# Partial sums of a seven-product block multiplication kept in PSUM instead of added on VectorE

## The chip, the cores and the metric

The kernel runs on one core of a Trainium2 chip. A core has a matrix engine (TensorE, in the profile PE for the matmuls and PEld for the loading of their weights), three engines for element-wise work (VectorE is DVE, ScalarE is ACT, GpSimd is POOL), and an engine that issues DMAs (SyncE, SP). Matmul results land in PSUM, which DVE and ACT read in this kernel; POOL works on SBUF alone. The metric is the device time of one execution in microseconds. Three runs of the kernel before took 1466.47 to 1467.98 us, median 1466.99 us.

## What is computed

The reference is a two-layer network on 1024 latent tokens (and 256 context tokens) of width 1024. What matters here are four matrix products, each of which the kernel does with one scheme:

```python
# layer 0, second half of the output projection's input comes from branch A
x  = x + gate * (concat([y_a, y_b]) @ ev_w_out)     # y_a part: "woa"
# layer 1 (w_grp and scale are folded with the first half of od_w_in)
u, g = split(h @ od_w_in)                           # "v" (folded) and "g"
y  = group_matmul(pool(u) - u, w_grp) * scale * silu(g)
x  = x + gate * (y @ od_w_out)                      # "wo": two halves of the 2048 inputs, "wo0" and "wo1"
out = rmsnorm(x, final_g)
```

## The kernel before

**Tiles.** Channels lie on the 128 partitions, tokens along the free dimension. A number in fp32 is split into a rounded high part and a low rest, and a product is three matmuls (high x high, high x low, low x high) of 128 x 128 weights on 128 x 512 data.

**A quad.** `quad` (L610) makes two output row tiles (m and m + 1) of all 1024 tokens, so four blocks of 128 x 512: (0,0), (0,1), (1,0) and (1,1), row tile and token half. Input and weight are cut in halves too, and a Strassen scheme in Winograd's form makes the four blocks from seven products instead of eight: products 1 to 7 take the operands `b11`, `b21`, `b22`, `t4`, `t1`, `t2`, `t3` in that order of their numbers. Each product is 12 matmuls (`prod`, L595), a quad is 84. Blocks are sums of products: (0,0) is 1 + 2, and the other three share the partial sum 1 + 6, and two of them also 1 + 6 + 7.

Before, the shared sums are made outside PSUM: ACT copies product 1 to an SBUF tile `s1` (L616); DVE adds product 6 to it into `s2` (L621) and product 6 + 7 to it into `s1` (L636); product 2 is accumulated on product 1 in PSUM tile `a`, product 7 on 6 in `b`, product 3 on 5 in `c`, and product 4 has its own tile `d`. ACT copies product 5 to `s3` (L629). Then `put` ends each block: (1,1) is `s3 + s1`, added on POOL; (1,0) is `s1 - d`, (0,1) is `s2 + c`, added on DVE. `quad` is called 26 times, for woa (4), v (8), g (8), wo0 (4) and wo1 (2), and the last two quads of wo1 have the same pattern written out in `last_half0` (L1182) and after it.

**What put does.** For v (`to_tokens`, L1011) it leaves the block in a tile that is pooled along the tokens on DVE; for g (`to_gate`, L1018) ACT applies SiLU, and DVE multiplies the two (L1057); for woa and wo0 (`added`, L802) DVE multiplies by the gate and adds the residual, which a DMA loads into one of two buffers (`xp`) and another stores; for the other quads of wo1 (`put`, L1102) the residual is already in SBUF (`gated`, L1090).

**Weights.** For each quad `wquad` (L567) loads two raw tiles (two buffers), makes the combinations that the seven products need, and splits each into high and low: ACT casts the high part (L94), DVE makes the low part of products 1 and 6, POOL of 2, 5, 7, 4 and 3 (L95). So the raw tiles of the next quad are loaded when POOL has done with those of the last one, and the loads stand in SP's queue between the stores of the results.

**Operands.** The operands of wo0 and wo1 are sums of y blocks that go through DRAM (`y_store` L952, `y_sums`, `y_operand` L969).

**Order.** A planner, not the source, sets the order of each engine's instructions: it simulates the program, starts what is ready, and prefers what has high priority (`tc.high_priority`, the readers of PSUM) or comes earlier in the source; `tc.issue_after` adds an order on one engine. Each engine then runs its list in that order. PSUM has four tiles for `a`, `b`, `c`, `d` (pool `pm`).

Of the kernel before, what the change touches and what calls it, by code (L numbers as in the profile page):

```python
# [20 lines left out]
KT = D // P  # L21
H = 512
# [28 lines left out]
BOPS = ("b11", "t2", "b21", "t1", "t3", "t4", "b22")  # L51
# [3 lines left out]
def body(ctx, tc, xT, ctxT, cc, ccol, modT, modW, win, gw, wout, wu, grp, wg, wo1, small, edge, ident, outT):  # L55
# [511 lines left out]
    def wquad(src, name, ring):  # L567
        raw = []
        for i in range(2):
            r = wpool.tile([P, D], F32, tag="wr", name=f"wr_{name}_{i}")  # L570
            loaded[0] = nc.sync.dma_start(r, src[i])
# [9 lines left out]
        p1 = op(a11, 1, nc.vector)  # L581
        s3 = ttile(f"ws_{name}")
        nc.vector.tensor_tensor(out=s3, in0=a11, in1=a21, op=sub)
        nc.vector.tensor_tensor(out=a21, in0=a21, in1=a22, op=add)
        nc.vector.tensor_tensor(out=a11, in0=a21, in1=a11, op=sub)  # L585
        p6 = op(a11, 6, nc.vector)
        p2 = op(a12, 2, nc.gpsimd)
        p5 = op(a21, 5, nc.gpsimd)
        p7 = op(s3, 7, nc.gpsimd)
        nc.vector.tensor_tensor(out=a12, in0=a12, in1=a11, op=sub)  # L590
        p4 = op(a22, 4, nc.gpsimd)
        p3 = op(a12, 3, nc.gpsimd)
        return p1, p2, p3, p4, p5, p6, p7
# [13 lines left out]

    EVAC = 1000

    def quad(w, name, ops, put, ahead=None):  # L610
        p1, p2, p3, p4, p5, p6, p7 = w
        a = psum(f"qa_{name}")
        prod(a, p1, ops["b11"], True, False)
        s1 = ttile(f"s1_{name}")
        with tc.high_priority(offset=EVAC):
            evac_a = nc.scalar.copy(s1, a)  # L616
        b = psum(f"qb_{name}")
        prod(b, p6, ops["t2"], True, False)
        s2 = ttile(f"s2_{name}")
        with tc.high_priority(offset=EVAC):  # L620
            evac_v = nc.vector.tensor_tensor(out=s2, in0=b, in1=s1, op=add)  # L621
# [3 lines left out]
        c = psum(f"qc_{name}")  # L625
        prod(c, p5, ops["t1"], True, False)
        s3 = ttile(f"s3_{name}")
        with tc.high_priority(offset=EVAC):
            nc.scalar.copy(s3, c)  # L629
        w = None  # L630
        if ahead is not None:
            with tc.issue_after(evac_a.ins), tc.issue_after(evac_v.ins):
                w = ahead()
        prod(b, p7, ops["t3"], False, True)
        with tc.high_priority(offset=EVAC):
            nc.vector.tensor_tensor(out=s1, in0=b, in1=s1, op=add)  # L636
# [4 lines left out]
        with tc.high_priority(offset=EVAC):  # L641
# [123 lines left out]
    for i in range(KH):  # L765
# [16 lines left out]
        nc.vector.tensor_tensor(out=t4, in0=t2, in1=b21, op=sub)  # L782
        split_op(ya, "t2", i, t2)
        split_op(ya, "t1", i, t1)
        for name, v in zip(BOPS[4:], (t3, t4, b22)):
            kept[name].append(v)
# [13 lines left out]


    def added(gate, m, i, h, x, y, op, dst=None):  # L802
        t = vtile(f"xp{m}_{i}_{h}")
        dst = t if dst is None else dst
        nc.sync.dma_start(t, x1_part[m + i][:, HALF[h]])
        if y is not None:
            eng = nc.gpsimd if (i, h) == (1, 1) else nc.vector
            eng.tensor_tensor(out=x, in0=x, in1=y, op=op)
        nc.vector.scalar_tensor_tensor(out=dst, in0=x, scalar=gate[:, 0, 2 * KT + m + i : 2 * KT + m + i + 1],  # L809
                                       in1=t, op0=mult, op1=add)  # L810
        nc.sync.dma_start(x1_part[m + i][:, HALF[h]], dst)
# [18 lines left out]
    def woa(m, w, ahead):  # L830
        def put(i, h, x, y, op):
            if (i, h) == (0, 0):
                for q in range(2):
                    x1[m + q] = xtile(f"x1_{m + q}")
            v = x1[m + i][:, HALF[h]]
            added(m0, m, i, h, x, y, op, v)
            square_acc(nacc[h][:, :H], v, (m, i) == (0, h), f"n1q{m}_{i}_{h}")
# [57 lines left out]
    for i in range(KH):  # L895
# [3 lines left out]
        t = block_sums(b11, b12, b21, b22, ttile(f"xt3_{i}"), nc.vector)  # L899
        split_x("t2", i, t["t2"], shift(KH + i), None)  # L900
        split_x("t1", i, t["t1"], None, nc.gpsimd)
        split_x("t3", i, t["t3"], dsh[:, i : i + 1], None)
        split_x("t4", i, t["t4"], None, nc.gpsimd)
        split_x("b22", i, b22, shift(KH + i), None)
# [46 lines left out]

    def y_store(m, name, v):  # L952
        part, i = divmod(m // 2, KH)
        nc.sync.dma_start(y_raw[part][name][:, i * H : (i + 1) * H], v)
# [9 lines left out]
    def y_sums(m):  # L964
        t = block_sums(*y_blocks(m), vtile(f"yt3_{m}"), nc.vector)
        for name in BOPS[1:2] + BOPS[3:6]:
# [30 lines left out]
    def wo1_weights(part, m):  # L997
        return wquad([wo1[m + i, part] for i in range(2)], f"wo{part}_{m}", wo1_ring)

    wo1_ring = wo_ring(iter(["x", "x", "x", "wh", "wl", "wh", "wl"] + ["wh", "wl", "d", "d"] * 14))  # L1000
    vps = []
    for m in range(0, NK, 2):
# [8 lines left out]
        def to_tokens(i, h, x, y, op):  # L1011
            if y is None:
                nc.scalar.copy(token[i][h], rows(x))
            else:
                eng = nc.gpsimd if (i, h) == (1, 1) else nc.vector
                eng.tensor_tensor(out=token[i][h], in0=rows(x), in1=rows(y), op=op)

        def to_gate(i, h, x, y, op):  # L1018
            v = ys[m + i][:, HALF[h]]
            if y is None:  # L1020
                nc.scalar.activation(v, x, AF.Silu)
            else:
                eng = nc.gpsimd if (i, h) == (1, 1) else nc.vector
                eng.tensor_tensor(out=v, in0=x, in1=y, op=op)
                nc.scalar.activation(v, v, AF.Silu)
# [22 lines left out]
        def first_weights():  # L1048
            w = wo1_weights(0, 0)
            y_operands(0, iter([xtile] * 7), BOPS[4:])  # L1050
            return w

        w = quad(wq, f"g{m}", bx, to_gate, first_weights if m == NK - 2 else None)
# [16 lines left out]

    for m in range(0, KT, 2):
        def put(i, h, x, y, op):
            added(m1, m, i, h, x, y, op)
# [16 lines left out]
    def gated(k, v, x):  # L1090
        return nc.vector.scalar_tensor_tensor(out=v, in0=x, scalar=m1[:, 0, 2 * KT + k : 2 * KT + k + 1],  # L1091
                                              in1=v, op0=mult, op1=add)

# [7 lines left out]
    for m in range(0, KT - 4, 2):  # L1101
        def put(i, h, x, y, op):  # L1102
            v = x1[m + i][:, HALF[h]]
            if y is not None:
                eng = nc.gpsimd if (i, h) == (1, 1) else nc.vector
                eng.tensor_tensor(out=x, in0=x, in1=y, op=op)
            gated(m + i, v, x)
            square_fin(m + i, h, slice(0, H), v)
# [73 lines left out]
    def last_half0(m, w, ahead=None):  # L1182
        p1, p2, p3, p4, p5, p6, p7 = w
        a = psum(f"qa_l{m}")
        prod(a, p1, ops["b11"], True, False)
        s1, s2 = ttile(f"s1_l{m}"), ttile(f"s2_l{m}")
        with tc.high_priority(offset=EVAC):
            evac_a = nc.scalar.copy(s1, a)
        b = psum(f"qb_l{m}")
        prod(b, p6, ops["t2"], True, False)  # L1190
        with tc.high_priority(offset=EVAC):
            evac_v = nc.vector.tensor_tensor(out=s2, in0=b, in1=s1, op=add)
        nxt = None
        if ahead is not None:
            with tc.issue_after(evac_a.ins), tc.issue_after(evac_v.ins):
                nxt = ahead()
        prod(a, p2, ops["b21"], False, True)
        with tc.high_priority(offset=EVAC):
            gated(m, x1[m][:, HALF[0]], a)
            fin_add(HALF[0], square(m, HALF[0]))  # L1200
        mm = prod(b, p7, ops["t3"], False, True)
        with tc.high_priority(offset=EVAC):
            gated(m, x1[m][:, HALF[1]], s2)
            nc.vector.tensor_tensor(out=s1, in0=b, in1=s1, op=add)
        d = psum(f"qd_l{m}")
        with tc.issue_after(mm.ins):
            mm = prod(d, p4, ops["t4"], True, True)
        with tc.high_priority(offset=EVAC):
            nc.vector.tensor_tensor(out=d, in0=s1, in1=d, op=sub)
            gated(m + 1, x1[m + 1][:, HALF[0]], d)  # L1210
            fin_add(HALF[0], square(m + 1, HALF[0]))
            vec = gated(m + 1, x1[m + 1][:, HALF[1]], s1)
# [143 lines left out]
```

## Time and profile before

| what | value |
|---|---|
| median of three runs | 1466.99 us |
| the profiled execution, its own time | 1463.63 us |
| its span, first to last instruction | 1461.8 us |
| mean granted TensorE clock | 0.961 |
| instructions of PE, DVE, ACT, POOL in the trace | 5664, 1445, 906, 398 |

The span falls into stages, by what TensorE works on: up to 763 us the projections and the recurrence of layer 0, which the change leaves alone; 763 to 854 the four quads of woa; 854 to 906 the folding of weights and the normalisation; 906 to 1254 the sixteen quads of v and g in eight pairs; 1254 to 1401 the four quads of wo0 and two of wo1; 1401 to 1445 the last two quads of wo1, and then the final normalisation. In a row of groups the columns are line, engine, operation, output <- inputs, shapes, count, then busy microseconds and mean nanoseconds of one, then idle time before it. In a row for a stretch they are the stretch, its length, and busy microseconds with the count for each engine, then the granted clock, the share of DMA time, and GB/s.

### The profile page before, as it was taken

Reading aid. Unit: us, or ns where it says so; the run is one execution under the profiler, and the core shown is the slowest. Engines: PE = TensorE matmul, PEld = TensorE weight load, DVE = VectorE, ACT = ScalarE, POOL = GpSimd, SP = SyncE. Lnnn points to the kernel's source line nnn. Section 1 sums busy time; section 2 is a strip of 40 time slices with the busy share of each in tenths; the row PEclk is TensorE's granted clock in tenths of the full one; section 3 lists DMA queues with packets and bytes.
Section 4 is the critical chain, followed back from the end, with each engine's and each line's share of the span. In section 5 each row is a group of like instructions: output and inputs, shape, how many; then the busy total and the mean of one; then the engine's idle time right before and its main releaser. Section 6 shows DMA issues by size and latency. Waiting matters only on the chain. (4 is left out here: it accounts for less than half of the span.)

```text
span 1461.8 us, 15892 instructions
## 1 busy us (share of the span) xinstructions
PE 1323.3 (91%) x5664; PEld 1060.8 (73%) x5664; DVE 1265.6 (87%) x1445; ACT 639.2 (44%) x906; POOL 739.9 (51%) x398
## 2 busy tenths in 40 slices
PE   7799989897999889999998989999998997798896
PEld 4478767776777677888886877778777775577675
DVE  7985889798879899997878859999999999986985
ACT  6443584466457624226334345433332223433542
POOL 5273654664557456425327446555435536445642
PEclk9999999999999999999999999999999999899998
DMA  9741212121211223443542475133342135457723
GB/s 362 251 116 39 63 37 73 65 65 34 75 51 52 71 94 119 133 146 120 190 137 98 158 219 169 56 129 129 116 137 86 66 116 173 151 187 241 244 91 115
DMA packets 82867, 181.80 MB, mean 124 GB/s; under 512 B 7778, under 2 KB 27618, under 8 KB 82788
## 3 DMA queue, kind: packets, MB, share of 16 engines
q1 hardware_dynamic: 74340, 176.60, 36.7%
q10 hardware_dynamic: 8448, 4.20, 1.0%
q8 instruction: 44, 0.72, 0.2%
q14 instruction: 35, 0.29, 0.1%
HBM read 136.72 MB, written 44.04 MB: 124 GB/s over the span
## 5 line engine op out<-in xcount | busy, mean ns | idle before, releaser
L681 DVE SCALAR_TENSOR_TENSOR conv<-u,sm,conv 128x1009 f32<-128x1009 f32 (+14 forms) x240 | 300.8, 1272 | 21.9 <-ACT conv L674 18.7
L95 POOL TENSOR_TENSOR wl_wu<-wr_wu,wh_wu 128x1024 fp32r<-128x1024 f32 x16 | 38.7, 2422 | 68.4 <-ACT wh_wu L94 68.4
L95 POOL TENSOR_TENSOR wq_wo<-wr_wo,wq_wo 128x512 fp32r<-128x512 f32 x32 | 49.7, 1558 | 43.8 <-ACT wq_wo L94 42.5
L95 POOL TENSOR_TENSOR wq_g<-wr_g,wq_g 128x512 fp32r<-128x512 f32 x32 | 55.0, 1735 | 31.6 <-ACT wq_g L94 31.6
L94 ACT CAST wq_v<-wr_v 128x512 fp32r<-128x512 f32 x48 | 28.2, 619 | 91.3 <-DVE wr_v L585 45.5
L520 PE MATMUL g<-uh,wh_gw 128*128 128x512 f32 (+1 forms) x96 | 40.1, 419 | 25.7 <-ACT g L523 16.3
L95 POOL TENSOR_TENSOR wq_v<-wr_v,wq_v 128x512 fp32r<-128x512 f32 x32 | 55.3, 1744 | 14.8 <-ACT wq_v L94 11.1
L94 ACT CAST wq_g<-wr_g 128x512 fp32r<-128x512 f32 x48 | 28.2, 619 | 78.7 <-DVE wr_g L585 28.4
L523 ACT ACTIVATE g<-g,sm 128x512 f32<-128x512 f32 (+1 forms) x96 | 53.4, 623 | 18.0 <-PE g L522 10.1
L242 PE MATMUL fold<-gh,wh_wu 128*128 128x512 f32 x128 | 53.6, 420 | 6.3 <-ACT wh_wu L94 6.3
L439 POOL TENSOR_TENSOR g<-g,uc 128x1280 f32<-128x1280 f32 x16 | 47.4, 2963 | 19.9 <-ACT g L523 19.9
L124 PE MATMUL gb<-h0h,wh_gb 128*128 128x512 f32 x128 | 51.7, 404 | 5.5 <-ACT sb L662 5.5
L243 PE MATMUL fold<-gl,wh_wu 128*128 128x512 f32 x128 | 52.8, 413 | 3.7 <-DVE gl L95 3.7
L444 POOL TENSOR_TENSOR g<-g,g 128x1280 f32<-128x1280 f32 x16 | 50.6, 3176 | 9.6 <-ACT g L443 9.6
L457 POOL TENSOR_TENSOR g<-g,g 128x1024 f32<-128x1024 f32 x8 | 19.1, 2387 | 70.6 <-DVE g L454 70.6
L445 DVE SCALAR_TENSOR_TENSOR g<-a,g 128x1280 f32<-128x1280 f32 x16 | 37.1, 2316 | 20.3 <-POOL g L444 20.3
L244 PE MATMUL fold<-gh,wl_wu 128*128 128x512 f32 x128 | 51.7, 413 | 2.7 <-POOL wl_wu L95 2.7
L126 PE MATMUL va<-h0h,wl_va 128*128 128x512 f32 x128 | 49.6, 391 | 3.1 <-POOL wl_va L95 3.1
L125 PE MATMUL gb<-h0l,wh_gb 128*128 128x512 f32 x128 | 51.4, 401 | 0.0
L126 PE MATMUL gb<-h0h,wl_gb 128*128 128x512 f32 x128 | 50.9, 399 | 0.0
L125 PE MATMUL wob<-ybl,wh_wob 128*128 128x512 f32 x128 | 50.3, 394 | 0.0
L126 PE MATMUL ga<-h0h,wl_ga 128*128 128x512 f32 x128 | 50.2, 392 | 0.0
(577 smaller groups left out, 4802.4 us busy)
## 6 DMA issues: line engine op xcount, KB each, us to landing
mod<-modT SPq DMA_DIRECT2D x28, 512.0 KB, 3.9
wr_wu<-wu SPq DMA_DIRECT2D x16, 512.0 KB, 4.1
x_part<-xp SPq DMA_DIRECT2D x32, 256.0 KB, 3.2
xp<-x_part SPq DMA_DIRECT2D x32, 256.0 KB, 4.1
mod<-modT SPq DMA_DIRECT2D x32, 256.0 KB, 3.5
wr_v<-wfold SPq DMA_DIRECT2D x16, 512.0 KB, 3.5
wr_g<-wg SPq DMA_DIRECT2D x16, 512.0 KB, 4.4
yr_t<-y_t SPq DMA_DIRECT2D x16, 512.0 KB, 5.8
```

Source lines behind the costliest of these rows:

```text
L94: return (nc.scalar.copy(hi, src), eng.tensor_tensor(out=lo, in0=src, in1=hi.bitcast(F32), op=sub))
L95: eng.tensor_tensor(out=lo, in0=src, in1=hi.bitcast(F32), op=sub))
L124: nc.tensor.matmul(ps, hi[:, kc], xh[k][:, cols], start=(k == 0), stop=False)
L125: nc.tensor.matmul(ps, hi[:, kc], xl[k][:, cols], start=False, stop=False)
L126: nc.tensor.matmul(ps, lo[:, kc], xh[k][:, cols], start=False, stop=(k == ks - 1))
L242: nc.tensor.matmul(ps, wh[:, kc], gh[i], start=(i == 0), stop=False)
L243: nc.tensor.matmul(ps, wh[:, kc], gl[i], start=False, stop=False)
L244: nc.tensor.matmul(ps, wl[:, kc], gh[i], start=False, stop=(i == 3))
L439: nc.gpsimd.tensor_tensor(out=ius[d], in0=ius[d], in1=uc, op=mult)
L444: nc.gpsimd.tensor_tensor(out=iu, in0=iu, in1=r, op=mult)
L523: nc.scalar.activation(t[:, a : a + n], ps[:, :n], AF.Sigmoid, bias=col(ob + d * KT + j))
L681: nc.vector.scalar_tensor_tensor(out=acp[:, a:b], in0=us[j][:, a + o : b + o], scalar=col(O_CONVW + 31 * j + k), in1=acp[:, a:b], op0=mult ...
```

## The change

The order of the products becomes 1, 5, 6, 2, 7, 3, 4 in the source. ACT copies product 1 from PSUM tile `a` into PSUM tile `b`, and products 6, 7 and 4 accumulate on that copy one after the other; after 6, after 7 and after 4 `b` holds a finished partial sum or block, and each is read before the next product is accumulated on it. There is no tile `d`: a quad has three PSUM tiles. Block (1,0) needs the sign of product 4 turned, so `t4` is made with its operands exchanged. `put` now gets a part: 0 and 1 for the two parts of blocks (1,1) and (0,1), None for a block that comes whole.

- woa and wo1: each part is multiplied by the gate and added to the residual by its own DVE instruction out of PSUM; woa loads the residual straight into its tile of `x1`.
- v, g and wo0: ACT copies part 0 to SBUF (`keep_part`), DVE adds part 1 to it. In v and g, block (1,0) now comes whole from PSUM to ACT.
- POOL adds nothing in a quad any more.

Beside that: `wquad` hands POOL product 5 first and 4 last (in the last four row tiles of wo1 product 4 first); the loads of weights for wo0 are ordered behind the last store of y; three of the operands of wo0 are ordered, on ACT, behind the last SiLU; the order of operands follows `BOPS`.

```diff
-BOPS = ("b11", "t2", "b21", "t1", "t3", "t4", "b22")
+BOPS = ("b11", "t1", "t2", "b21", "t3", "b22", "t4")
...
-        eng.tensor_tensor(out=b21, in0=b11, in1=b21, op=sub)
+        eng.tensor_tensor(out=b21, in0=b21, in1=b11, op=sub)
...
     def quad(w, name, ops, put, ahead=None):
         p1, p2, p3, p4, p5, p6, p7 = w
-        a = psum(f"qa_{name}")
+        a, c, b = psum(f"qa_{name}"), psum(f"qc_{name}"), psum(f"qb_{name}")
         prod(a, p1, ops["b11"], True, False)
-        s1 = ttile(f"s1_{name}")
         with tc.high_priority(offset=EVAC):
-            evac_a = nc.scalar.copy(s1, a)
-        b = psum(f"qb_{name}")
-        prod(b, p6, ops["t2"], True, False)
-        s2 = ttile(f"s2_{name}")
+            evac = nc.scalar.copy(b, a)
+        prod(c, p5, ops["t1"], True, False)
         with tc.high_priority(offset=EVAC):
-            evac_v = nc.vector.tensor_tensor(out=s2, in0=b, in1=s1, op=add)
+            put(1, 1, c, 0)
+        prod(b, p6, ops["t2"], False, False)
+        with tc.high_priority(offset=EVAC):
+            put(0, 1, b, 0)
         prod(a, p2, ops["b21"], False, True)
         with tc.high_priority(offset=EVAC):
-            put(0, 0, a, None, None)
...
-        prod(b, p7, ops["t3"], False, True)
+        prod(b, p7, ops["t3"], False, False)
         with tc.high_priority(offset=EVAC):
-            nc.vector.tensor_tensor(out=s1, in0=b, in1=s1, op=add)
-        with tc.high_priority(offset=EVAC):
-            put(1, 1, s3, s1, add)
-        d = psum(f"qd_{name}")
-        prod(d, p4, ops["t4"], True, True)
-        with tc.high_priority(offset=EVAC):
-            put(1, 0, s1, d, sub)
+            put(1, 1, b, 1)
         prod(c, p3, ops["b22"], False, True)
         with tc.high_priority(offset=EVAC):
-            put(0, 1, s2, c, add)
+            put(0, 1, c, 1)
+        prod(b, p4, ops["t4"], False, True)
+        with tc.high_priority(offset=EVAC):
+            put(1, 0, b, None)
...
+    def keep_part(parts, name, i, x):
+        parts[i] = ttile(f"s{i}_{name}")
+        nc.scalar.copy(parts[i], x)
...
-        def put(i, h, x, y, op):
+        def put(i, h, x, part):
+            if part == 0:
+                keep_part(parts, f"wo0_{m}", i, x)
+                return
+            t = vtile(f"xp{m}_{i}_{h}")
+            nc.sync.dma_start(t, x1_part[m + i][:, HALF[h]])
+            if part == 1:
+                s = x if i == 0 else parts[i]
+                nc.vector.tensor_tensor(out=s, in0=x, in1=parts[i], op=add)
+                x = s
+            gated(m + i, t, x)
+            nc.sync.dma_start(x1_part[m + i][:, HALF[h]], t)
...
-                return wo1_weights(0, m + 2)
+                with tc.issue_after(stored[0].ins):
+                    return wo1_weights(0, m + 2)
...
-        w = quad(wq, f"g{m}", bx, to_gate, first_weights if m == NK - 2 else None)
+        w = quad(wq, f"g{m}", bx, to_gate, (lambda: wo1_weights(0, 0)) if m == NK - 2 else None)
+        if m == NK - 2:
+            with tc.issue_after(silu[0].ins):
+                y_operands(0, iter([xtile] * 7), BOPS[4:])
```

More of the change, by code (lines that the diff above doesn't have):

```diff
@@ L781, in body @@
         nc.vector.tensor_tensor(out=t2, in0=b22, in1=t1, op=sub)
-        nc.vector.tensor_tensor(out=t4, in0=t2, in1=b21, op=sub)
+        nc.vector.tensor_tensor(out=t4, in0=b21, in1=t2, op=sub)
         split_op(ya, "t2", i, t2)
         split_op(ya, "t1", i, t1)
-        for name, v in zip(BOPS[4:], (t3, t4, b22)):
+        for name, v in zip(BOPS[4:], (t3, b22, t4)):
             kept[name].append(v)
@@ L830, in woa @@
     def woa(m, w, ahead):
-        def put(i, h, x, y, op):
[L832 to L837, printed above, removed]
+        for q in range(2):
+            x1[m + q] = xtile(f"x1_{m + q}")
+        def put(i, h, x, part):
+            v, dr = x1[m + i][:, HALF[h]], x1_part[m + i][:, HALF[h]]
+            if part != 1:
+                nc.sync.dma_start(v, dr)
+            nc.vector.scalar_tensor_tensor(out=v, in0=x, scalar=m0[:, 0, 2 * KT + m + i : 2 * KT + m + i + 1],
+                                           in1=v, op0=mult, op1=add)
+            if part != 0:
+                nc.sync.dma_start(dr, v)
+                square_acc(nacc[h][:, :H], v, (m, i) == (0, h), f"n1q{m}_{i}_{h}")
         return quad(w, f"woa{m}", ya, put, ahead)
@@ L965, in y_sums @@
         t = block_sums(*y_blocks(m), vtile(f"yt3_{m}"), nc.vector)
-        for name in BOPS[1:2] + BOPS[3:6]:
+        for name in ("t1", "t2", "t3", "t4"):
             y_store(m, name, t[name])
@@ L997, in wo1_weights @@
     def wo1_weights(part, m):
-        return wquad([wo1[m + i, part] for i in range(2)], f"wo{part}_{m}", wo1_ring)
+        return wquad([wo1[m + i, part] for i in range(2)], f"wo{part}_{m}", wo1_ring,
+                     part == 1 and m >= KT - 4)
     wo1_ring = wo_ring(iter(["x", "x", "x", "wh", "wl", "wh", "wl"] + ["wh", "wl", "d", "d"] * 14))
-    vps = []
+    vps, silu = [], [None]
     for m in range(0, NK, 2):
```

119 lines of the change are left out of this document (53 added, 66 removed).

## The prediction

> **What bounds the kernel now.** I read the page's busy shares first, then a table of the stages, the busiest pair of quads, TensorE's waits, and last the chain that feeds the weights.
>
> ```profile
> span 1461.8 us, 15892 instructions
> PE 1323.3 (91%) x5664; PEld 1060.8 (73%) x5664; DVE 1265.6 (87%) x1445; ACT 639.2 (44%) x906; POOL 739.9 (51%) x398
> ```
> ```profile
> core 0: us, PE busy (x) PEld busy (x) DVE busy (x) ACT busy (x) POOL busy (x), PEclk, DMA share, GB/s
> 763.45:853.86 90.41, 81.60 (x340) 63.84 (x339) 74.29 (x73) 38.59 (x65) 51.60 (x33) 0.98 0.43 135
> ...
> 905.58:953.00 47.42, 41.89 (x169) 33.02 (x168) 44.58 (x52) 25.77 (x44) 26.65 (x26) 0.93 0.26 84
> 953.00:1202.60 249.60, 234.75 (x1010) 190.77 (x1009) 232.64 (x314) 73.28 (x133) 117.70 (x71) 0.99 0.34 111
> 1202.60:1254.57 51.97, 41.08 (x170) 32.29 (x168) 49.60 (x54) 18.96 (x30) 27.73 (x15) 0.97 0.49 159
> 1254.57:1400.80 146.23, 127.19 (x508) 100.62 (x507) 121.09 (x118) 61.52 (x93) 85.99 (x50) 0.93 0.60 203
> 1400.80:1445.23 44.43, 41.80 (x201) 34.44 (x199) 33.75 (x45) 16.88 (x31) 11.82 (x9) 0.96 0.15 48
> ```
> ```profile
> 993.65:1032.50 38.85, 38.68 (x169) 31.38 (x168) 37.09 (x54) 10.89 (x20) 17.08 (x11) 1.00 0.39 127
> 1032.50:1075.50 43.00, 39.96 (x169) 32.62 (x168) 38.26 (x54) 13.87 (x26) 21.05 (x14) 0.96 0.37 118
> ```
>
> TensorE and VectorE run side by side and both are nearly full; in the six middle pairs VectorE is busy for 93% (232.64 of 249.60) and TensorE for 94%. The pair from 993.65 has no stall worth the name: 38.85 us, so 19.4 for a quad and 0.23 for a matmul. That is the floor. What a stage takes over it is what the change can win, for the number of matmuls stays. The excess is 249.60 - 6 x 38.85 = 16.5 in the middle pairs, 13.1 in the pair from 1202.60, 8.6 in the one from 905.58, 146.23 - 6 x 19.4 = 29.8 in the four wo0 and two wo1 quads, and 90.41 - 340 x 0.23 = 12.2 in woa.
>
> TensorE's waits, first from 905 to 1240 us, then from 1240 to 1446; columns: us in all, times, longest.
>
> ```profile
> PE qa_v L599 <- ACT s_v L616: 9.7, 4, 3.0
> PE qb_v L599 <- DVE s_v L621: 3.8, 2, 2.4
> ...
> PE qb_g L599 <- DVE s_g L621: 2.6, 3, 1.4
> PE qc_g L599 <- DVE vp L1016: 2.1, 1, 2.1
> ```
> ```profile
> PE qb_wo L599 <- DVE s_wo L621: 5.2, 2, 3.9
> PE qb_wo L599 <- ACT wq_wo L94: 4.7, 1, 4.7
> PE qb_g L599 <- DVE s_g L621: 3.7, 1, 3.7
> ```
>
> The readers of PSUM stand in these rows: product 2 waits for ACT's copy of product 1 (L616), product 7 for VectorE's add on product 6 (L621), 8 times and 15.3 us, 1.9 each.
>
> **The change part by part.** First VectorE and POOL (two windows, 905 to 1254 and 1254 to 1462; then one row from 763 to 854).
>
> ```profile
> L1016 POOL TENSOR_TENSOR vp<-s_v,s_v 128x512 f32<-128x512 f32 x8 | 13.3, 1659 | 39.3 <-ACT wq_g L94 35.5 <-DVE s_v L636 3.8
> ...
> L621 DVE TENSOR_TENSOR s_v<-qb_v,s_v 128x512 f32<-128x512 f32 x8 | 5.5, 684 | 0.0
> ...
> L616 ACT COPY s_g<-qa_g 128x512 f32<-128x512 f32 x8 | 4.7, 581 | 3.2 <-PE qa_g L602 3.2
> ```
> ```profile
> L809 DVE SCALAR_TENSOR_TENSOR xp<-s_wo,m,xp 128x512 f32<-128x512 f32 x12 | 14.7, 1229 | 9.8 <-DMA xp<-x_part 6.7 <-POOL s_wo L808 3.0
> L809 DVE SCALAR_TENSOR_TENSOR xp<-qa_wo,m,xp 128x512 f32<-128x512 f32 x4 | 3.0, 741 | 0.4 <-DMA xp<-x_part 0.4
> ```
> ```profile
> L809 DVE SCALAR_TENSOR_TENSOR x<-s_woa,m,xp 128x512 f32<-128x512 f32 x9 | 11.9, 1317 | 1.4 <-DMA xp<-x_part 1.3
> ```
>
> - v and g: VectorE has four adds in a quad before, two after; 16 x 2 x 0.68 = 21.8 us less, of it 12 x 2 x 0.68 = 16.3 in the middle pairs.
> - woa: a quad has four adds, three gated sums from SBUF and one from PSUM, 4 x 0.68 + 3 x 1.32 + 0.74 = 7.4; after, six gated sums out of PSUM, 6 x 0.74 = 4.4. Four quads: 12 less.
> - wo0: 4 x 0.68 + 3 x 1.23 + 0.74 = 7.15 before; two adds, three gated sums from PSUM and one from SBUF after, 1.36 + 2.22 + 1.23 = 4.8. Four quads: 9.4 less. The two wo1 quads lose 5.8 (as woa), the last two about 3.
> - VectorE in all: 52 us less. POOL: 26 adds x 1.66 = 43 less. Neither is the time won: work that TensorE did not wait for wins nothing, and only the excess above can go.
> - ACT: 22 copies more by the order of its instructions, x 0.58 = 12.8 us. ACT is 44% busy and its readers of PSUM have priority, so I cost them at nothing; if a copy stands behind a cast that waits, as in the L616 row, it costs up to 3.0 each.
>
> POOL's add has a second price. Rows of SP from 1040 to 1085, then of POOL from 1070 to 1084 (start, duration):
>
> ```profile
> 1042.07 0.88 SPq L571 DMA_DIRECT2D wr_g<-wg  x2
> 1061.17 2.12 SPq L571 DMA_DIRECT2D wr_v<-wfold  x2
> 1084.03 0.88 SPq L571 DMA_DIRECT2D wr_g<-wg  x2
> ```
> ```profile
> 1073.09 1.80 POOL L1024 TENSOR_TENSOR y<-s_g,s_g 128x512 f32<-128x512 f32 x1 [10.14 <-ACT wq_v L94]
> 1074.85 2.55 POOL L95 TENSOR_TENSOR wq_v<-wr_v,wq_v 128x512 fp32r<-128x512 f32 x2
> 1077.34 1.76 POOL L95 TENSOR_TENSOR wq_v<-ws_v,wq_v 128x512 fp32r<-128x512 f32 x1
> 1079.06 3.97 POOL L95 TENSOR_TENSOR wq_v<-wr_v,wq_v 128x512 fp32r<-128x512 f32 x2
> ```
>
> A load to the next one of its kind takes 41.96 us, three more than the floor of a pair: raw buffers come free only when POOL has done five splits, and the add of 1.80 stands ahead of them. It goes, so this cycle can come to the floor. VectorE gains here too:
>
> ```profile
> L590 DVE TENSOR_TENSOR wr_g<-wr_g x8: 1762/1766/1781, 936.8 to 1231.1; 128x512 f32<-128x512 f32 x8
> ...
>   POOL wq_v L95: 7.3, 6
> ```
>
> An SBUF-only add that takes 0.68 elsewhere takes 1.77 beside POOL, and waits 7.3 us for it; the splits stay, so the most of this stays.
>
> What a stall costs beside itself:
>
> ```profile
> 1040.00:1043.40 3.40, 0.38 (x2) 0.00 (x0) 3.40 (x6) 1.10 (x2) 1.07 (x1) 1.00 0.82 284
> 1043.40:1047.00 3.60, 3.59 (x9) 2.85 (x10) 2.75 (x8) 0.62 (x1) 0.00 (x0) 0.53 0.91 303
> ```
>
> After TensorE was idle for 3.0 of 3.4 us, the granted clock was 0.53 for the next 3.6 us: 9 matmuls where the floor has 15.6, 1.5 us lost. The Trainium skill ("TensorE: Matmul & The Clock Gate", "Part 1: The HAM clock gate (the "warmup" mystery)") has the half rate after an idle window of about 3.4 us; the row agrees in the rate, with a gap a little shorter. By that rule, waits of 1.9 us cost no clock.
>
> The new waits. Products 6, 7 and 4 are now accumulated on what a reader has just to have taken. By the order of TensorE's instructions, most quads of v and g run product 4 of the last quad behind product 1 of the next, so that 14 matmuls (3.2 us) lie between product 7 and 4, and 22 (5 us) between 6 and 7, for a reader of 0.58 to 0.74 us. Before, 22 to 24 lay there for L621, and TensorE waited for 8 of its 22 instances all the same (the row with L616 is the like for ACT). No row shows a slack of 14. The bounds: below nothing, since these waits take the place of L621's (-15.3); above, 26 x 1.9 = 49. I take +5, two or three such waits: the reader is first in VectorE's queue by priority and VectorE has 16.3 / 6 = 2.7 us less to do in a pair. Behind a waiting product 4 stand the 72 matmuls of the next quad's other products, and behind those every reader of that quad.
>
> The wo0 quads, by the page's rows of DMA issues and by the tile `xp` from 1250 to 1400 us:
>
> ```profile
> xp<-x_part SPq DMA_DIRECT2D x32, 256.0 KB, 4.1
> ...
> yr_t<-y_t SPq DMA_DIRECT2D x16, 512.0 KB, 5.8
> ```
> ```profile
> DMA to landing us min/median/max: 2.0/4.1/7.5
> ```
>
> Before, VectorE freed three of four PSUM tiles by adds that need no residual; now the gated sums that follow read PSUM tiles `b` and `c` after the residual has landed, 4.1 us after issue, in two buffers. A block's sum may wait for that, and the tile with it.
>
> The other edits go together. `t4` with its sign turned is one instruction for one. `wquad` hands POOL the same five splits in another order; the raw tiles are free after the last either way, and product 4's weights, now last, are wanted a quad's 72 matmuls (16.6 us) after product 1's, while the four splits ahead of it take about 8 (rows of POOL above); without that cover, a late split costs its 1.8. Residuals of woa land in `x1` itself: the same DMAs, 458 before and after, and no buffer to wait for. The loads of wo0's weights (two a quad) stand on SP behind the last store of y and whatever that store waits for, and three operands of wo0, each with a load of 512 KB (5.8 us to land) and a cast, on ACT behind the last SiLU: nothing of theirs is ahead of the gates any more, and the first products of wo0 may be late in their stead. The 4.7 us wait for L94 is the size of such a wait; bounds -4.7 and +4.7, taken as zero, since the three operands belong to the last products of a quad.
>
> The sum, by stage: middle pairs -13 of 16.5 (with 2.7 us less VectorE work than now, a pair is slower than the one at the floor only by the clock and the weights; 0.6 is left for them in each); pair from 1202.60 -6 of 13.1 (VectorE 49.60 of 51.97 busy there, with sums of y that stay); first pair -2 (operands bind it); wo0 and wo1 -8 of 29.8 (the L621 rows and the 3.0 of POOL); woa -4 of 12.2; the last quads -2. Together -35, and +5 for the new waits: -30. The profiled execution took 1463.6 and the median is 3.4 above it: 1467 - 30 = 1437. Its own range, 1415 to 1455: all the excess of the middle pairs and the wo stage halved below, a third of the sum above.
>
> **The rivals.**
> - wo0 gives it back. Four quads whose tiles wait for a residual, 4 x 4.1 = 16 us, for it: the row `xp<-x_part` 6.7 of idle VectorE; against it: loads can be issued well ahead. Then 1453, and at 7.5 a load about 1467.
> - Slower: product 4 waits for the reader of `b` in every quad. From 35 / 26 = 1.35 us a quad the gain is gone; at 1.9 (the mean of L621's waits) it is -35 + 49 = +14, 1481, and if every second one also costs 1.5 of clock, 1500. For it: 14 matmuls are fewer than the 22 that did not suffice 8 times, and VectorE stays 91% busy (216.3 of 236.6 in the middle pairs) with instructions of 1.77 in its way; against it: it takes two of those ahead of the reader, 3.5 us, to use up the slack.
> - The change doesn't do what it says: the adds taken away were hidden, the weights' cycle sets the pace and stays at 42, and the median stays within 0.2% (2.9 us, about what a measurement here can tell), 1467.
>
> The same Trainium skill page ("A second HAM failure mode: psum-queue depth-cycling") has short idle times between groups of matmuls wear down the clock. The middle pairs, with such waits, had 0.99; it would come on top of the second rival.
>
> **How the numbers follow.** My forecast 0.57, wo0 0.15, the slower rival 0.23, no change 0.05. Faster: 0.57 + 0.15 = 0.72. The range for 8 in 10 takes in the slower rival at 1.9 a quad, to 1482, and goes down to 1412; outside are the rival with clock losses and a stage at its floor everywhere.
>
> **What would show it.** Right: no rows of TensorE waiting for VectorE's readers over 5 us in all; pairs of v and g at 39 to 40 us; VectorE near 1213 us busy and POOL near 697; the raw loads 39 to 40 apart. Wrong: a row of `qb` waiting for a DVE or ACT reader some 20 times; granted clock under 0.96; xp rows with idle VectorE ahead of them; or pairs still at 42 with the wait moved to the weights (L94, L95).

## The result and the profile after

The changed kernel takes 1462.11 us (median of 11 runs, 1458.64 to 1467.11), the kernel before 1467.35 us (11 runs beside them, 1464.92 to 1470.05). The ratio is 0.9963, with a 95% interval of 0.9952 to 0.9973: 5.2 us less, a gain clear of the noise, and a sixth of the 30 us predicted. The profiled executions took 1463.63 before, one of the shorter ones, and 1462.24 after, so the two traces show only 1.4 us of the difference; what they compare well is where the waits lie.

The page's busy shares after:

```profile
PE 1320.8 (90%) x5664; PEld 1060.3 (73%) x5664; DVE 1212.2 (83%) x1389; ACT 652.9 (45%) x928; POOL 687.8 (47%) x372
```

The work went as predicted: VectorE is busy for 1265.6 - 1212.2 = 53.4 us less and POOL for 52.1 less. TensorE, with the same 5664 matmuls, ends hardly earlier. By stage, with the limits at the first matmul of product 1. First v and g, and wo0 with two wo1 quads, in the kernel before; then, in the changed kernel, the second and the fifth pair of v and g, and the same two stages:

```profile
905.58:1254.57 348.99, 317.73 (x1346) 256.09 (x1344) 326.82 (x418) 118.00 (x207) 172.09 (x111) 0.98 0.35 114
1254.57:1397.48 142.91, 123.87 (x493) 97.85 (x492) 117.77 (x116) 59.74 (x90) 82.67 (x48) 0.93 0.61 208
```
```profile
946.54:984.96 38.42, 38.37 (x169) 31.45 (x168) 31.40 (x44) 14.63 (x27) 14.38 (x10) 1.00 0.39 131
1065.28:1121.01 55.73, 46.93 (x193) 37.93 (x192) 47.54 (x68) 17.19 (x31) 19.05 (x13) 0.91 0.29 95
...
906.36:1254.52 348.16, 317.01 (x1333) 255.37 (x1332) 299.19 (x388) 130.23 (x228) 139.25 (x94) 0.96 0.34 114
1254.52:1394.97 140.45, 117.12 (x481) 94.17 (x480) 104.47 (x100) 59.56 (x90) 75.03 (x41) 0.94 0.62 212
```

In v and g VectorE loses 27.6 us of work (326.82 to 299.19), and the row is 0.8 us shorter. But the rows of the two kernels do not hold the same matmuls: the changed kernel runs product 4 of a quad behind the first products of the next one, across the limit. The count of weight loads (PEld) is 1332 in v and g against 1344 before, and 480 against 492 in the other stage, so 12 matmuls, 2.8 us at the floor's 0.23, are missing from each. With them neither stage has won anything. Equal counts give a fair comparison: the first 1848 weight loads from v on, up to the last two quads of wo1, and then those two quads, first before, then after:

```profile
905.58:1400.20 494.62, 444.31 (x1849) 356.19 (x1848) 447.31 (x535) 179.39 (x299) 257.48 (x160) 0.96 0.42 141
1400.20:1445.23 45.03, 42.40 (x203) 34.96 (x201) 34.35 (x45) 17.01 (x32) 12.42 (x9) 0.96 0.14 47
```
```profile
906.36:1403.13 496.77, 442.29 (x1849) 356.29 (x1848) 410.68 (x495) 194.37 (x325) 217.38 (x137) 0.95 0.42 140
1403.13:1443.43 40.30, 40.30 (x203) 33.98 (x201) 24.45 (x37) 16.61 (x30) 9.08 (x7) 1.00 0.15 52
```

With 36.6 us less work on VectorE, the stages from v to wo1 take 2.1 us more. What the changed kernel wins in these traces it wins in the last two quads, 4.7 us: the kernel before waits 2.6 us there for a reader (L1188, below), and the next 13 matmuls take 4.60 us, at a granted clock of 0.63, where the floor has 3.0. Measured in the same way, the last two quads take 45.0 to 45.4 us in the three kernels of this document that have them as before, and 40.3 to 41.3 in all the others.

The second pair runs at the floor, as the prediction has it for all of the middle ones. The fifth, from 1065.28, takes 55.73 with 192 weight loads, 24 more than a pair has; without these, at 0.23 each, 50.2. TensorE's waits, over the whole span after:

```profile
PE qb_v L606 <- DVE vp L1021: 21.7, 6, 8.0
...
PE qb_wo L606 <- DVE s_wo L1091: 9.8, 2, 5.4
...
PE qb_wo L606 <- DVE x L1076: 5.1, 1, 5.1
...
PE qb_wo L606 <- ACT s_wo L652: 3.0, 1, 3.0
```

All four are what the change adds: product 4 or 7 waits until a reader has taken the partial sum on which it accumulates (L1021 is the v quad's add on product 7, ahead of product 4). Together 39.6 us. What they replace is as large. Beside the rows of before that the prediction shows, its trace had these:

```profile
PE qa_wo L599 <- DVE s_wo L636: 3.7, 1, 3.7
...
PE qa_wo L599 <- ACT s_wo L616: 3.0, 2, 1.9
...
PE qa_l L599 <- ACT s_l L1188: 2.6, 1, 2.6
...
PE qb_g L599 <- DVE s_v L636: 1.5, 1, 1.5
```

From v on, the waits for the readers at L616, L621, L636, L1016 and L1188 were 12.7 + 15.3 + 5.2 + 2.1 + 2.6 = 37.9. The old waits went, as predicted, and new ones came.

Why VectorE was late shows in its own waits, from 906 to 1254 us:

```profile
DVE y L561 <- DMA y_b<-y: 14.8, 6, 5.4
DVE wq_v L95 <- ACT wq_v L94: 8.1, 7, 2.1
DVE mod L205 <- DMA mod<-modT: 7.7, 4, 3.3
```

Neither DMA wait is there in that stretch of the trace before. L561 is the last of the sums of y blocks, `t4`: it writes over block (1,0) and must wait until that block's store has read it. One of the six, on VectorE, SP and TensorE (start, duration):

```profile
1172.23 0.74 DVE L1061 SCALAR_TENSOR_TENSOR y<-vp,sm,y 128x512 f32<-128x512 f32 x1
1176.32 0.69 DVE L561 TENSOR_TENSOR y<-y,y 128x512 f32<-128x512 f32 x1 [3.35 <-DMA y_b<-y]
1176.93 0.69 DVE L586 TENSOR_TENSOR ws_g<-wr_g,wr_g 128x512 f32<-128x512 f32 x1
...
1184.45 3.27 DVE L927 TENSOR_TENSOR ws<-ws 128x616 f32<-128x616 f32 x3
1187.64 0.68 DVE L1021 TENSOR_TENSOR vp<-qb_v,s_v 128x512 f32<-128x512 f32 x1
```
```profile
1173.00 0.32 SPq L955 DMA_DIRECT2D y_b<-y  x1
```
```profile
1185.13 0.39 PE L609 MATMUL qa_g<-x_b11h,wq_g 128*128 128x512 f32 x1
1188.37 0.50 PE L606 MATMUL qb_v<-x_t4h,wq_v 128*128 128x512 f32 x1 [2.86 <-DVE vp L1021]
```

The gate is multiplied on at 1172.23, the store goes out at 1173.00, and VectorE stands for 3.35 us. Behind it in its queue lie the sums of weights, the pooling, and the reader at 1187.64; TensorE, at product 4 since 1185.5, waits 2.86. Product 4 is now the last of a quad, so block (1,0) is the last to be gated and stored. And TensorE runs it later than the source has it: product 4 of a g quad ends 5.6 to 16.0 us after the next pair has begun, where in the kernel before it ends 2.6 us ahead of that. So its gate stands close ahead of `t4` in VectorE's queue, here directly, and `t4` is reached before the store is through. The matmuls after this wait are slow, too:

```profile
1185.52:1188.37 2.85, 0.00 (x0) 0.00 (x0) 2.82 (x4) 0.72 (x2) 2.85 (x2) 1.00 0.15 19
1188.37:1192.79 4.42, 4.42 (x13) 3.52 (x14) 4.32 (x8) 0.62 (x1) 0.48 (x1) 0.65 0.63 224
```

13 matmuls in 4.42 us at a granted clock of 0.65; at the floor's 0.23 they take 3.0.

### The profile page after: what moved, and what is told of

Same layout as the page of the kernel before. It is cut to its first block, busy times and chain, and to the rows that moved or that the text cites. A ratio compares the mean times of both kernels' runs of the same rounds, so it can differ in the third digit from the quotient of the medians.

```text
span 1460.4 us, 15770 instructions
## 1 busy us (share of the span) xinstructions
PE 1320.8 (90%) x5664; PEld 1060.3 (73%) x5664; DVE 1212.2 (83%) x1389; ACT 652.9 (45%) x928; POOL 687.8 (47%) x372
## 5 line engine op out<-in xcount | busy, mean ns | idle before, releaser
L95 POOL TENSOR_TENSOR wq_v<-wr_v,wq_v 128x512 fp32r<-128x512 f32 x32 | 50.2, 1583 | 89.7 <-ACT wq_v L94 89.2
L95 POOL TENSOR_TENSOR wq_g<-wr_g,wq_g 128x512 fp32r<-128x512 f32 x32 | 49.0, 1546 | 90.9 <-ACT wq_g L94 90.8
L95 POOL TENSOR_TENSOR wq_wo<-wr_wo,wq_wo 128x512 fp32r<-128x512 f32 x32 | 49.1, 1542 | 60.0 <-ACT wq_wo L94 50.2
L523 ACT ACTIVATE g<-g,sm 128x512 f32<-128x512 f32 (+1 forms) x96 | 53.4, 624 | 16.4 <-PE g L522 8.5
L94 ACT CAST wq_wo<-wr_wo 128x512 fp32r<-128x512 f32 x48 | 28.8, 620 | 51.6 <-DMA wr_wo<-wo 15.1
```

Source lines behind the costliest of these rows:

```text
L94: return (nc.scalar.copy(hi, src), eng.tensor_tensor(out=lo, in0=src, in1=hi.bitcast(F32), op=sub))
L95: eng.tensor_tensor(out=lo, in0=src, in1=hi.bitcast(F32), op=sub))
L523: nc.scalar.activation(t[:, a : a + n], ps[:, :n], AF.Sigmoid, bias=col(ob + d * KT + j))
```

## The experiments

Theory A, formed on these rows: VectorE's queue is held by waits for DMAs, mainly the store of block (1,0), and what stands behind it, the readers of PSUM, comes late. Theory B, the prediction's own rival: 14 matmuls between products 7 and 4 are too few, whatever holds VectorE. Times are medians beside runs of the kernel before on the same chip; whether two kernels differ is judged by their ratios to it, 0.9963 for the changed kernel, and differences in us are those of the medians.

**t4 in a tile of its own**

```diff
-        t = block_sums(*y_blocks(m), vtile(f"yt3_{m}"), nc.vector)
+        b11, b12, b21, b22 = y_blocks(m)
+        t3, t4 = vtile(f"yt3_{m}"), ttile(f"yt4_{m}")
...
+        nc.vector.tensor_tensor(out=t4, in0=b21, in1=b11, op=sub)
+        t = dict(t2=b11, t1=b12, t3=t3, t4=t4)
```

> The changed kernel, but the sum t4 of four y blocks is written to a tile of its own instead of over block (1,0), so VectorE need not wait until the store of that block has been read. Theory A (VectorE is held by DMAs: since product 4 is now last, block (1,0) is stored last and its in-place sum waits 14.8 us in 6 places, and everything behind it on VectorE, the readers of PSUM too, is late): that wait goes to zero, product 4's waits for the reader of product 7 in v (21.7 us in 6) fall under 8 us, and the time falls by 8 to 15 us, to 1447 to 1454. Theory B (the 14 matmuls between products 7 and 4 are too few for a VectorE with this load, whatever it waits for): product 4's waits stay above 15 us and the time within 4 us of 1462.

1453.64 us, ratio 0.9899 (0.9869 to 0.9929), 8.5 less than the changed kernel. The wait for the store is gone; TensorE's longest waits from 905 to 1254 us now (the second row is the first quad of wo0, already begun):

```profile
PE qb_v L606 <- DVE vp L1027: 10.1, 3, 6.4
PE qa_wo L609 <- DVE wq_wo L95: 6.2, 1, 6.2
PE qb_g L606 <- DVE y L1035: 5.1, 2, 3.8
```

The order of TensorE's instructions in v and g is that of the changed kernel, 14 matmuls between products 7 and 4 and all, and product 4's wait in v halves. It does not fall under 8, as A expected, and some of it is met in g instead (L1035). The time is as A has it.

**Product 4 in a PSUM tile of its own**

```diff
-        prod(b, p4, ops["t4"], False, True)
-        put(1, 0, b, None)
+        put(1, 0, b, 0)
+        d = psum(f"qd_{name}")
+        prod(d, p4, ops["t4"], True, True)
+        put(1, 0, d, 1)
```

> The changed kernel, but product 4 goes to a PSUM tile of its own, and block (1,0) is made of two parts as (1,1) and (0,1) are: product 4 waits for no reader, at 26 more instructions on ACT or VectorE. Theory A: the waits for DMA on VectorE remain (over 20 us of idle VectorE in v and g), TensorE's wait moves to the next reader or to the weights, and the time falls by 3 to 8 us. Theory B: product 4's waits (21.7 us in v, 9.8 in wo0) go and nothing takes their place: 15 to 25 us less, 1437 to 1447.

1469.32 us, ratio 1.0005 (0.9990 to 1.0020): 6 to 7 us slower than the changed kernel, which neither theory had. Product 4 waits for no reader any more. But VectorE has 26 instructions more (1415 for 1389), and the part of block (1,0) is one more copy in ACT's queue, where the copies of parts in v wait 22.6 us for VectorE's adds; the casts of weights in the same queue come late. TensorE's and VectorE's waits in v and g:

```profile
PE qc_g L606 <- ACT wq_g L94: 7.8, 3, 4.5
```
```profile
DVE wq_g L95 <- ACT wq_g L94: 21.4, 7, 6.3
DVE ws L930 <- ACT vp L1020: 13.3, 6, 4.1
```

Against B: with the dependence gone, the time is not won. The planner also ordered TensorE anew here (part of product 4 runs ahead of 7), so the run says no more than that, and that the copies make the casts late is argued from the rows, not shown.

**Both edits** (the two diffs above in one kernel)

> Both edits together: t4 in a tile of its own, and product 4 in its own PSUM tile. Theory A: 10 to 18 us less than the changed kernel, not more than 5 beyond the first edit alone. Theory B: as the second edit alone, within 4 us of it.

1467.40 us, ratio 0.9990 (0.9974 to 1.0007). The gain of the first edit does not appear; the casts hold VectorE as in the run before (`ws` behind ACT's copies, 20.9 us). A miss for A's sum.

**v and g as before** (`quad_old` is the `quad` of the kernel before; `to_tokens`, `to_gate` and the weights of v and g go with it)

```diff
-        quad(wv, f"v{m}", bx, to_tokens)
+        quad_old(wv, f"v{m}", bx, to_tokens)
...
-        w = quad(wq, f"g{m}", bx, to_gate, (lambda: wo1_weights(0, 0)) if m == NK - 2 else None)
+        w = quad_old(wq, f"g{m}", bx, to_gate, (lambda: wo1_weights(0, 0)) if m == NK - 2 else None)
```

> The changed kernel with the quads of v and g as before (partial sums in SBUF, POOL's add, products in the order 1, 6, 2, 5, 7, 4, 3, weights in the old order); woa, wo0, wo1 and the last quads as changed. By the two profiles v and g take 348 to 349 us either way, so theories A and B both have the gain of 5 us come from elsewhere, and the time within 3 us of 1462. The rival to that: the profile of the kernel before was of one of its shorter executions, and v and g did win; then 1466 to 1469.

1468.58 us, ratio 1.0001 (0.9983 to 1.0019). The time is the rival's: without the changed v and g nothing is won. Its reason, that v and g did win, is not shown by that: the experiment with woa and wo as before, below, wins nothing either.

**The modulation sums behind the pooling** (on top of t4 in its own tile)

```diff
-                mod_tile(m1, 1, n + q, raw, (cL2,), raw)
+                mods1.append((n + q, raw))
...
+        for n, raw in mods1:
+            with tc.issue_after(pooled.ins):
+                mod_tile(m1, 1, n, raw, (cL2,), raw)
```

> The changed kernel with t4 in a tile of its own, and beside that the modulation sums (L205, two a pair up to the fifth pair, whose loads VectorE waited 8.4 us for in the run with t4 alone) stand behind the pooling of the pair on VectorE. Theory A (whatever holds VectorE makes product 4 wait): the waits for these loads fall under 3 us, the longest wait of product 4 (6.4 us, in the fifth pair) goes, and the time falls by 4 to 8 us against the run with t4 alone, to 1446 to 1450. Theory B (too few matmuls between product 7 and 4): within 3 us of 1453.6, with the same waits of product 4.

1455.43 us, ratio 0.9908 (0.9880 to 0.9935), the time that B expected. The wait for `mod` is gone and the longest wait of product 4 with it, but the wait only changes places (the planner also changed TensorE's order here):

```profile
PE qb_g L606 <- DVE y L1035: 10.2, 4, 3.7
...
PE qb_v L606 <- DVE vp L1027: 4.0, 2, 2.5
```

10.1 + 5.1 in v and g became 4.0 + 10.2. So A holds for the store, not for whatever makes VectorE wait.

**The kernel before with products 3 and 4 exchanged** (and the order in which their weights are made)

```diff
+        prod(c, p3, ops["b22"], False, True)
+        put(0, 1, s2, c, add)
         d = psum(f"qd_{name}")
         prod(d, p4, ops["t4"], True, True)
         put(1, 0, s1, d, sub)
-        prod(c, p3, ops["b22"], False, True)
-        put(0, 1, s2, c, add)
```

> The kernel before with one thing of the change: products 3 and 4 change places (and their weights), so block (1,0) is the last of its quad, and nothing else. Theory A: the in-place sum t4, which never waited in the kernel before, now waits on VectorE for the store of that block, some 5 to 15 us in all, and the time rises by 3 to 10 us, to 1470 to 1478. The rival (the order of the blocks is of no matter, the load of VectorE is): 1467, within 3 us.

1469.73 us, ratio 1.0010 (0.9998 to 1.0021): no change that can be told. Of VectorE's waits in v and g, those for y blocks and their stores:

```profile
DVE y L1057 <- ACT y L1025: 10.5, 7, 1.9
...
DVE y L561 <- DMA y_b<-y: 0.8, 1, 0.8
```

The exchange alone does not make `t4` wait: VectorE reaches it 0.8 us early once. A's expectation of a slower kernel was wrong. But the edit did not make block (1,0) as late as the change does. In the order that the planner made, product 4 of a g quad ends 0.2 us after the next pair has begun, with only its last two matmuls behind product 3, against 5.6 to 16.0 us in the changed kernel. So whether the 14.8 us came from that lateness or from less work on VectorE is not shown.

**The kernel before with t4 in a tile of its own** (the edit of the first experiment)

```diff
-        t = block_sums(*y_blocks(m), vtile(f"yt3_{m}"), nc.vector)
...
+        nc.vector.tensor_tensor(out=t4, in0=b11, in1=b21, op=sub)
+        t = dict(t2=b11, t1=b12, t3=t3, t4=t4)
```

> A control: the kernel before, with t4 in a tile of its own. It did not wait for that store, so by theory A nothing changes: 1467, within 3 us. If the tile itself, or the order that the planner makes with it, were what made the changed kernel faster by 8 us, this one would be as well: 1459.

1485.19 us, ratio 1.0114 (1.0087 to 1.0142), 17 us slower, which neither expectation had. The tile comes from the same four buffers as the partial sums, and is held until its store is done:

```profile
DVE ws_g L583 <- DMA y_t<-yt: 7.7, 5, 2.7
```

These waits are 7.7 us of the 17; where the rest comes from was not tried. The control shows that the tile itself is no gain, but also that it is no neutral edit. So the first experiment was repeated without it, last below.

**Product 1's low weights of wo on POOL** (on top of t4 in its own tile)

```diff
-        p1 = op(a11, 1, nc.vector)
+        p1 = op(a11, 1, nc.gpsimd if name[:3] in ("wo0", "wo1") else nc.vector)
```

> The changed kernel with t4 in a tile of its own, and in wo0 and wo1 the low part of product 1's weights is made on POOL and not on VectorE, so VectorE does not stand waiting for a cast of weights that have just landed (12.7 us in three places in the run with t4 alone). If late weights hold VectorE and so the readers of PSUM: 4 to 8 us less than that run, 1446 to 1450. If the weights themselves are late, TensorE waits for them instead: within 3 us of 1453.6, or longer, as POOL's split is slower (1.3 us against 0.69).

1450.37 us, ratio 0.9882 (0.9858 to 0.9907); 3.3 us less than without, with intervals that overlap, so between the two expectations. Of VectorE's 12.7 us of waiting for the casts of weights 1.0 is left, and it waits 14.3 us for the residuals (9.9 without the edit).

**Product 4 of v behind products 1 and 5 of g** (`last` is the v quad's product 4 with its `put`, run inside the g quad)

```diff
-        prod(c, p5, ops["t1"], True, False)
+        m5 = prod(c, p5, ops["t1"], True, False)
...
+            with tc.issue_after(m5.ins):
+                last()
```

> The changed kernel, but product 4 of each v quad stands behind products 1 and 5 of the g quad that follows, so that 26 matmuls and not 14 lie between product 7 and 4 (2.7 us more for the reader); VectorE's own work is the same, and it still waits for the store of block (1,0). If 14 matmuls are simply too few: five of the six waits of product 4 in v (21.7 us) shrink by 2.7 us each, and v and g take 10 to 13 us less, about 1450. If a late VectorE is what costs, and TensorE meets it at another place (the next reader, the weights): waits of other products for VectorE appear, and the time is within 4 us of 1462.

1462.42 us, ratio 0.9947 (0.9932 to 0.9962), an interval that overlaps the changed kernel's. Product 4 waits no more. Product 5 of g does, for the add on product 3, which frees its PSUM tile and stands behind the add on product 7 in VectorE's queue (one line, L1029, makes both; each time product 5 starts 0.15 us after the second):

```profile
PE qc_g L606 <- DVE vp L1029: 23.3, 6, 8.1
```

Six times, 23.3 us, where product 4 had six times, 21.7. More slack alone wins nothing that can be told: VectorE's adds are late by more than a quad's PSUM tiles can bridge, and TensorE meets them at the next tile that it needs. This is against B, as long as VectorE waits for the store (12.6 us here).

**woa and wo as before**

```diff
-        w = quad(w, f"wo0_{m}", yops[0], put, nxt)
+        w = quad_old(w, f"wo0_{m}", yops[0], put, nxt)
...
-        w = quad(w, f"wo1_{m}", yops[1], put, ahead)
+        w = quad_old(w, f"wo1_{m}", yops[1], put, ahead)
```

> The changed kernel with the quads of woa, wo0 and the first two of wo1 as before (with their additions on VectorE and POOL and their order of weights); v, g and the last two quads as changed. The run with v and g as before gave 1468.6, so the changed woa and wo bring nothing by themselves; if the parts add up, this one is within 3 us of the changed kernel, 1459 to 1465. If the changed woa and wo are worth the 14 us of the prediction, only masked in that run, this one is slower by 5 us or more: 1467 and up.

1468.52 us, ratio 0.9991 (0.9977 to 1.0004). The parts do not add up: either half of the change alone gives nothing, both give 0.37%. The last two quads, changed in both mixed kernels, keep what they won (40.3 and 41.2 us). The loss is in the stages from v to wo1, for the same 1848 weight loads as above; first v and g as before, then this kernel:

```profile
905.55:1409.48 503.93, 449.49 (x1850) 359.20 (x1848) 440.21 (x531) 182.90 (x304) 249.82 (x152) 0.95 0.42 139
```
```profile
908.29:1409.04 500.75, 446.23 (x1850) 358.42 (x1848) 415.23 (x506) 193.10 (x325) 226.45 (x143) 0.95 0.42 140
```

That is 503.9 and 500.8 us against 494.6 before and 496.8 changed. Some of the distance to the kernel before is its execution, which was 3.7 us under the median (1463.63 against 1467.35); the changed kernel's was not. What costs a mixture of old and new stages 4 to 7 us more than the changed kernel wasn't tried further.

**Three edits together** (the diffs of t4's tile, of the weights on POOL, and of product 4 behind product 5, in one kernel)

> The changed kernel with three edits: t4 in its own tile, product 1's low weights of wo on POOL, and product 4 of v behind products 1 and 5 of g. If slack and the wait for the store are two causes that add up: below the 1450.4 of the first two by 3 us or more, 1443 to 1447. If both cure the same waits: within 3 us of 1450.

1446.01 us, ratio 0.9834 (0.9810 to 0.9858), the fastest of all: 16 us less than the changed kernel and 24 less than the kernel before. It is 4.4 us less than without the move of product 4, as expected if slack and the store are two causes that add up; the intervals of the two runs meet at 0.9858. So the slack, which won nothing while VectorE waited for the store, seems to be worth something without that wait, and theory B is not excluded. TensorE still waits 13.5 us in v and g for the add on product 3.

**t4 behind the sums of weights**

```diff
-            y_sums(m - 2)
+            t = y_sums(m - 2, ("t1", "t2", "t3"))
         wq = wquad([wg[m + i] for i in range(2)], f"g{m}", ring_x)
+            with tc.issue_after(wsum[0].ins):
+                nc.vector.tensor_tensor(out=t["t4"], in0=t["t4"], in1=t["t2"], op=sub)
```

> The changed kernel with the in-place sum t4 moved behind the sums of the g quad's weights on VectorE (some 3 us of work and a cast later); no new tile, no other change, the order of TensorE's instructions in v and g is that of the changed kernel. It repeats the first experiment without its extra tile, which made the kernel before 17 us slower. If VectorE's wait for the store of block (1,0) is the cause: that wait (14.8 us) falls under 4 us, product 4's waits in v (21.7 us) to half or less, and the time to 1452 to 1458. If it was the tile, or the planner's new order with it, that made the first experiment faster: within 3 us of 1462.

1456.70 us, ratio 0.9927 (0.9907 to 0.9947), 5.4 us less than the changed kernel, with intervals that do not touch. In v and g:

```profile
PE qb_v L607 <- DVE vp L1030: 13.5, 5, 9.2
```

No wait for the store is left, with no new tile and TensorE's order in v and g unchanged but for the last quad of g. Product 4's wait falls from 21.7 to 13.5, not to the half that was expected. With the tile or without it, taking VectorE's wait for the store away is worth 5 to 9 us: that part of theory A is shown.

## Why the prediction was wrong

The sign was right and the range held the time; the size was not, -5 for -30. The sign is in part luck: in the traces the gain lies in the last two quads, which had 2 of the 35 us, and the stages that had the other 33 won nothing.

- **The work removed** was sized rightly: 52 us predicted for VectorE and 53.4 measured, 12.8 and 13.7 for ACT's copies. POOL lost 52.1 for 43.
- **"+5 for the new waits"** is the term that failed: they are 39.6 us, near the upper bound of 49 that stood beside it, and as much as the waits that went (37.9). The sum does not close with it: -35 + 39.6 is a loss of 5, and 5 were won, so the -35 was not right in itself either. The prediction's own slower rival came about in part: product 4 waited in six of eight v quads, not in every quad, but up to 8.0 us and not 1.9.
- **The reason given for +5** failed with it: "the reader is first in VectorE's queue by priority and VectorE has 2.7 us less to do in a pair". Each engine runs a fixed list, and less work does not bring the reader forward if an instruction ahead of it waits for a DMA. More slack alone was tried (26 matmuls for 14), and the wait moved to product 5.
- **"`t4` with its sign turned is one instruction for one"** is the step that overlooked the cause. The number of instructions is the same; what moved is the block that it overwrites, to the end of its quad and into the next pair. The text counted what the order of the products does to TensorE, and not what it does to the gate, the store and the sum that follow the last block.
- **By stage:** v and g were to win 21, wo0 and wo1 8; with equal counts of matmuls they lost 2.1 together. Among the pairs of v and g, the second won 2.2 (40.65 to 38.42) and the fifth lost 8 (42.13 to 50.2). woa was to win 4: from its first matmul to the first of v it is 1.1 us slower (142.13 to 143.27). The last quads were to win 2 and won 4.7.
- **The weights' cycle** came to the floor only where VectorE was not held: loads of `wr_v` are 39.5 us apart from 978.64 to 1018.16, and 43.4 from 1058.83 to 1102.24.

```profile
978.64 2.14 SPq L572 DMA_DIRECT2D wr_v<-wfold  x2
1018.16 2.14 SPq L572 DMA_DIRECT2D wr_v<-wfold  x2
1058.83 2.14 SPq L572 DMA_DIRECT2D wr_v<-wfold  x2
1102.24 1.55 SPq L572 DMA_DIRECT2D wr_v<-wfold  x2
```

- **The wo0 rival** did not come: VectorE waited 2.2 us for a residual where it had waited 7.0.
- **Two smaller figures** do not come out: the words for the lower end of the range give 1422 (-45.4 in place of -35, and nothing for the waits), not 1415; and the traces have 456 DMA issues on SP, not 458, though as many before as after, which is what the argument needs.

Shown is that VectorE's wait for the store was 5 to 9 us of what was missed. Three things stay open. With the waits for the store and for `mod` gone, TensorE still waits 14.2 us in v and g for VectorE's adds, and no run shows which instruction ahead of them would have to move. What made `t4` wait, the lateness of product 4 or the lighter VectorE, is not separated. And why the stages from v to wo1 take longer in the mixed kernels than in the changed one is not known.

## What to carry to other kernels

When products or blocks change their order, follow the last one all the way: its reader, its store, and every instruction that writes over it again; an in-place sum that never waited can become the head of an in-order queue. Work taken off an engine is worth nothing while that engine waits in order for something else. If TensorE waits for a late reader, look first at what stands ahead of the reader in its own queue; moving the product that waits handed the wait to the next PSUM tile here. And before the times of a stage are compared across two orders of work, count the matmuls between the limits.

## What was not expected of the hardware and its queues

A wait of 2.85 us, shorter than the 3.04 of the prediction's row, was followed by 4.42 us at a granted clock of 0.65. The Trainium skill ("TensorE: Matmul & The Clock Gate", "Part 1: The HAM clock gate (the "warmup" mystery)") has the half rate follow an idle window of about 3.4 us; here, in the changed kernel as in the one before, shorter waits already cost 1.4 to 1.5 us beside themselves, so both rows agree with the page's rate, and neither with its length. Nor does the length alone tell: a wait of 2.98 us in the changed kernel was followed by matmuls at full clock.

```profile
1273.82:1276.80 2.98, 0.00 (x0) 0.00 (x0) 1.45 (x2) 2.98 (x6) 2.98 (x2) 1.00 0.87 243
1276.80:1281.00 4.20, 3.72 (x15) 2.74 (x15) 4.20 (x3) 2.37 (x3) 4.20 (x2) 1.00 0.05 17
```

And the kernel before with `t4` in one 128 x 512 tile from a ring of four, held until its store had landed, took 17 us longer; 7.7 us of waits for such stores are on VectorE's record.
